# A two-layer decoder trunk on one core: a fourth buffer for split weights, embedding products in another bank, a new order of the attention steps

## The chip, the cores and the metric

The kernel runs on one core of a Trainium2 chip. The metric is the device time of one execution in microseconds (us). The engines of the core are TensorE (PE, its weight loads PEld), VectorE (DVE), ScalarE (ACT), GpSimd (POOL) and SyncE (SP, which issues the DMAs).

## The reference, cut to what matters

Two layers over 256 tokens of width 1024. Each is a feed-forward block, a mixer, a second feed-forward block and a gated embedding; the mixer of layer 0 is stick-breaking attention with 16 heads of 64, that of layer 1 a causal pooling over windows of 2, 4, 8 and 16 tokens.

```
for i in range(DEPTH):
    x = x + 0.5 * swiglu(rms_norm(x, norm_ffn1[i]), w_ffn1_gu[i], w_ffn1_down[i])
    h = rms_norm(x, norm_mix[i])
    mix = stick_breaking_attention(h, ...) if i % 2 == 0 else multiscale_pool_mixer(h, ...)
    x = x + mix
    x = x + 0.5 * swiglu(rms_norm(x, norm_ffn2[i]), w_ffn2_gu[i], w_ffn2_down[i])
    gate = jax.nn.sigmoid(rms_norm(x, norm_ple[i]) @ w_ple_gate[i])
    x = x + gate * (p[i] @ w_ple_proj[i])
```

All inputs are float32. Attention takes, for each query, scores z of the earlier keys, the running sum of log sigmoid(-z) from the key to the query, and weights exp(log sigmoid(z) + that sum).

## The kernel before

Activations lie with features on partitions: `x` is 8 chunks of 128 features by 256 tokens, inside the tile `gx`. Every float32 operand of a matmul is split into a high part (rounded to fp32r) and a low part (the rest), and each product is three matmuls, high x high, high x low and low x high (`mm3`, L183). So the weights must be split on the chip.

**The stream of weights.** All weights are cut into 163 units of 128 x 2048 floats (1 MB), in the order of use. `load(u)` (L122) fetches unit u into one of three `raw` buffers, from SP's queue. `divide(u)` (L139) makes its parts `wh` (on ScalarE, or on DVE for the first pieces where the table `SPLIT` says so) and `wl` (raw minus wh, on DVE, or on POOL for the last pieces where the table says so). The table's triple is (pieces, pieces whose `wh` is made by DVE, pieces whose `wl` is made by POOL); a unit without an entry has (2, 0, 0), which is pieces of 1024 columns. The pool `wpool` (L89) has three buffers each for `wh` and `wl`. `unit(u)` (L166) is called by whoever uses a unit: it issues loads up to u + 3 and the divisions of u and u + 1. `ahead()` (L174) issues the division of the unit two behind the newest in use. A division's instructions can run only when a buffer is free, that is when PE has used up the unit that held it.

**The order of the work.** PE and SP run in the order of the program. The instructions of ScalarE, DVE and POOL are put in an order by the compiler's own scheduler when the kernel is built, by readiness and priority; marked parts have high priority, the divisions do not. On the chip each engine then runs its instructions in that order.

**PSUM.** Eight banks: four named `mm`, two `z`, one `st`, one `o`. `next_bank()` (L106) takes every third from `z`, the others from `mm`.

**Feed-forward** (`ffn`, L400). Units 0 to 21 of a block hold gate and up weights, one pair of 128 columns each: 48 matmuls of 256 columns a unit (`project`). `gated` (L412) scales by the norm's factor `r`, takes silu and product on ScalarE and DVE, and splits the result into `hx`. The last 11 units are the down projection. From the second block on the first two units are worked on side by side, chunk by chunk of the incoming `x` (`Opening`, L346), so that PE can begin before the last chunk is ready; `statistics()` (L311) then takes the sum of squares `acc` through PE (parts `ah` and `al` into bank `st`) and makes `r`. The second block of layer 1 gets an opening of one unit, which `pooling` has begun.

**Attention** (`attention`, L463). The list `HEADS` (L70) is PE's order, written by hand: q, k, v steps are six matmuls of 512 columns each of a projection (group of heads, then chunk); T is the transposition of the queries and keys of a pair of heads into bank `st`, read out into `kh`, `kl`, `qh`, `ql`; C the scores into both `z` banks, after which ScalarE and DVE make the softplus `spv` and its parts `sph` and `spl`; S the running sums on PE, after which the weights `pwv`, `pwh`, `pwl` are made; G the sum of the values into bank `o`, read out into `oh` and `ol`; W one input chunk of the output projection (24 matmuls of 256 columns, into all four `mm` banks); E a quarter of layer 0's embedding product `p @ w_ple_proj` (12 matmuls) into bank `st`, copied into `proj` by ScalarE (L756); N the token statistics; A a call of `ahead()`. A group of k is normalized into `y` (L518) before T can use it.

**Units.** Layer 0: feed-forward 0 to 32; attention 33 to 49, of which W0 and W1 use 45, E 46, W2 to W7 use 47 to 49; feed-forward 50 to 82; embedding gate 83 to 86 (`embed`, L762). Layer 1: feed-forward 87 to 119; embedding product 120; pooling 121 to 125; feed-forward 126 to 158; gate 159 to 162. Only feed-forward, the gate and one place each in attention and pooling call `ahead()`.

Of the kernel before, what the change touches and what calls it, by code (L numbers as in the profile page):

```python
# [16 lines left out]
P = 128  # L17
D = 1024
S = 256
# [36 lines left out]
}  # L56


# [11 lines left out]
HEADS = """  # L70
q00 q01 q02 q03 q04 q05 N q06 q07 k00 k01 k02 k03 k04 k05 k06 k07
v00 v01 v02 v03 T0 v04 v05 C0 v06 T1 v07 q10 q11 S0 q12 q13 C1 G0 q14 T2 q15 q16 q17 S1
k10 k11 C2 G1 k12 T3 k13 k14 k15 S2 k16 k17 C3 G2 v10 v11 v12 v13 T4 S3 v14 v15 v16 C4 G3
v17 T5 W0 S4 E0 C5 G4 W1 T6 E1 S5 E2 C6 G5 W2 T7 W3 S6 E3 C7 G6 W4 W5 S7 W6 A G7 W7
"""


# [1 line left out]
def trunk(ctx: ExitStack, tc: tile.TileContext, gxT, pT, wts, outT):  # L79
# [39 lines left out]

    raw, split = {}, {}  # L120

    def load(u):  # L122
        if u >= UNITS or u in raw:
            return
        t = wpool.tile([P, UNIT], F32, tag="raw", name=name("raw"))
        if u == 0:
            for a, b in FIRST:
                lo, hi = (G_COLS if a else 0) + a * S, G_COLS + b * S
                nc.sync.dma_start(gx[:, lo:hi], gxT[:, lo:hi])
                c = slice(a * UNIT // 8, b * UNIT // 8)  # L130
                nc.sync.dma_start(t[:, c], wts[u, :, c])
        else:
            pieces = 4 if u == 1 else 1
            n = UNIT // pieces
            for i in range(pieces):
                nc.sync.dma_start(t[:, i * n : (i + 1) * n], wts[u, :, i * n : (i + 1) * n])
        raw[u] = t

    def divide(u, only=None):  # L139
        if u >= UNITS or (u in split and only is None):  # L140
            return
        load(u)
        if u not in split:
            split[u] = (
                wpool.tile([P, UNIT], F32R, tag="wh", name=name("wh")),
                wpool.tile([P, UNIT], F32R, tag="wl", name=name("wl")),
            )
        h, lo = split[u]
        pieces, on_dve, on_pool = SPLIT.get(u, (2, 0, 0))
        cuts = [(i * UNIT // pieces, (i + 1) * UNIT // pieces) for i in range(pieces)]  # L150
        if u == 0:
            cuts = [(a * UNIT // 8, b * UNIT // 8) for a, b in FIRST]
        for i, (a, b) in enumerate(cuts):
            if only not in (None, i):
                continue
            c = slice(a, b)
            if i < on_dve:
                nc.vector.tensor_copy(h[:, c], raw[u][:, c])
            else:
                nc.scalar.activation(h[:, c], raw[u][:, c], AF.Copy)  # L160
            eng = nc.gpsimd if i >= len(cuts) - on_pool else nc.vector
            eng.tensor_sub(lo[:, c], raw[u][:, c], f(h[:, c]))  # L162
# [10 lines left out]

    def ahead():  # L174

        divide(newest[0] + 2)

    def tile_of(u0, i):
        h, lo = unit(u0 + i // 16)
# [220 lines left out]
    def ffn(n, u0, last_norm, aside=None, before=None, opening=None):  # L400

        if n:
            opening = opening or Opening(u0, (xh, xl), list(range(NC)))
        opened = len(opening.banks) if n else 0
        if n:
            opening.step()
            statistics()
        with tc.tile_pool(name=name("ffn"), bufs=1) as pool:
            hx = pool.tile([P, 2, NFF, S], F32R, name=name("hx"))
            hh, hl = hx[:, 0], hx[:, 1]  # L410

            def gated(j, ps):  # L412
                s = tmp.tile([P, S], F32, tag="s", name=name("s"))
                nc.vector.tensor_mul(s, ps[:, :S], r)  # L414
                nc.scalar.activation(s, s, AF.Silu)
                nc.vector.tensor_mul(s, s, ps[:, S:])
                nc.scalar.activation(hh[:, j], s, AF.Copy)
                nc.vector.tensor_sub(hl[:, j], s, f(hh[:, j]))

            waiting = list(enumerate(opening.banks)) if n else []  # L420
            for w in waiting:
                gated(*w)
            waiting = []
            for j in range(opened, NFF):
                ps = next_bank()
                if u0 + j == 0:
                    for k in range(NC):
                        for i in range(2):
                            mm3(
                                ps[:, i * S : (i + 1) * S], tile_of(0, 2 * k + i),  # L430
                                (xh[:, k], xl[:, k]), i + k == 0, k == NC - 1,
                            )
                else:
                    project(u0 + j, ps, (xh, xl))
                waiting.append((j, ps))
                if n == 0 and j == 1:
                    before()
                    statistics()
                if n or j:
                    for w in waiting:  # L440
                        gated(*w)
                    waiting = []
                ahead()
                if j == 4 and aside is not None:
                    aside()
            r_ffn = r
            begin_norm()
            for d in range(NC):
                ps = next_bank()
                for k in range(NFF):  # L450
                    w = tile_of(u0 + NFF, d * NFF + k)
                    mm3(ps[:, :S], w, (hh[:, k], hl[:, k]), k == 0, k == NFF - 1)
                t = tmp.tile([P, S], F32, tag="s", name=name("s"))
                with tc.high_priority():
                    nc.vector.scalar_tensor_tensor(
                        out=t, in0=ps[:, :S], scalar=0.5, in1=r_ffn, op0=ALU.mult, op1=ALU.mult
                    )
                    nc.vector.tensor_add(x[:, d], x[:, d], t)  # L458
                    last_norm(d, d == 0)
        return u0 + UNITS_FFN  # L460


    def attention(u0, layer, embedding):  # L463
        uo = (u0 + 12, u0 + 14, u0 + 15, u0 + 16)
        with tc.tile_pool(name=name("attn"), bufs=1) as pool:
# [151 lines left out]
            for step in HEADS.split():  # L617
                what, n = step[0], step[1:]
                if what in "qkv":
                    group = "qkv".index(what) + 3 * int(n[0])  # L620
                    k = int(n[1])
                    if k == 0:
                        banks = [bank("mm"), bank("mm")]
                    project_tokens(u0 + 2 * group, banks, (k,))
                    if k == NC - 1 and what == "v":
                        c = slice(int(n[0]) * 512, int(n[0]) * 512 + 512)
                        keep_tokens(vh[:, :, c], vl[:, :, c], banks, rc)
                    elif k == NC - 1:
                        normalize((what, int(n[0])), banks, epsms)
                elif what == "N":  # L630
                    rc, epsms = token_scales()
                elif what == "A":
                    ahead()
                elif what == "E":
                    embedding(int(n), tag="st")
                else:
                    {"T": transpose, "C": scores, "S": stick, "G": gather, "W": w_o}[what](int(n))
            begin_norm()
# [99 lines left out]

    def embedding_of(u0, pool):

        proj = pool.tile([P, NC, S], F32, name=name("proj"))

        def some(*which, tag=None):
            for i in which:
# [53 lines left out]
    with tc.manual_schedule(engines={mybir.EngineType.PE, mybir.EngineType.SP}):  # L798
# [6 lines left out]
        for layer in range(DEPTH):  # L805
# [19 lines left out]
                2 * layer, u, norm_after(1, layer, ("ffn1", layer)), aside,  # L825
                None if layer else rest_of_squares,
            )
            with tc.tile_pool(name=name("embed"), bufs=1) as pool:
                if layer == 0:
                    proj, embedding = embedding_of(u + 13, pool)  # L830
                    u, opening = attention(u, layer, embedding), None
                else:
                    proj, embedding = embedding_of(u, pool)
                    u, opening = pooling(u, layer, embedding)
                u = ffn(
                    2 * layer + 1, u, norm_after(3, layer, ("ffn2", layer)), opening=opening
                )
                if layer + 1 < DEPTH:
                    u = embed(u, proj, norm_after(0, layer + 1, ("ple", layer)))
                else:  # L840
                    u = embed(u, proj, None)
        assert u == UNITS


# [93 lines left out]
```

## Time and profile before

| what | us |
|---|---|
| median of 3 runs | 1008.12 (1006.88 to 1009.69) |
| the profiled execution | 1007.78 |
| its span in the trace | 1006.1 |

All times in a trace row are microseconds from the start of the span, unless marked ns. The profiled execution is 1.7 us longer than its span, which is the work around it. A group of instructions is named by line, engine, operation and tiles, out<-in; since the matmuls are recorded by one helper, all of them have line L111. In the timeline a bracket names the idle time ahead of an instruction and what ended it.

### The profile page before, as it was taken

What the parts mean: (1) busy time and instruction counts of PE and PEld (TensorE: products, weight loads), DVE (VectorE), ACT (ScalarE), POOL (GpSimd) and SP (SyncE); (2) the same over time, 40 slices, a digit from 0 to 9 for tenths busy, and PEclk for the clock granted to TensorE, in tenths of its full rate; (3) what the DMA queues carried; (4) which work ended last, traced back from release to release, by engine and by line L of the source; (5) the groups of instructions that cost most, each with busy time, mean ns of one, the idle gap of its engine ahead of it and who ended that gap; (6) DMA issues with size and microseconds to landing.
All of it is one profiled execution on the core that took longest, in us unless ns stands there. A gap on an engine that the chain in (4) does not pass through costs nothing.

```text
span 1006.1 us, 18488 instructions
## 1 busy us (share of the span) xinstructions
PE 977.6 (97%) x7710; PEld 951.6 (95%) x7710; DVE 670.5 (67%) x1107; ACT 527.6 (52%) x885; POOL 122.5 (12%) x183
## 2 busy tenths in 40 slices
PE   8999999999998999999999999999999899999997
PEld 8999999987777999999999999999998899999997
DVE  7966565678966876565658676565666766565565
ACT  5654544457756674444438554443456654444442
POOL 4300002500000000000240070000220000000262
PEclk9999999999989999999999999999999999999999
DMA  7754554543321364555543555555554355545531
GB/s 252 262 209 169 198 178 171 208 168 125 129 100 66 133 238 176 192 186 188 189 175 121 209 212 177 189 188 184 194 174 162 126 203 175 193 184 189 190 126 42
DMA packets 26292, 174.77 MB, mean 174 GB/s; under 512 B 2912, under 2 KB 3680, under 8 KB 5600
## 3 DMA queue, kind: packets, MB, share of 16 engines
q1 hardware_dynamic: 26208, 173.59, 48.1%
q8 instruction: 60, 0.98, 0.4%
q14 instruction: 24, 0.20, 0.1%
HBM read 172.53 MB, written 1.05 MB: 173 GB/s over the span
## 4 chain that ended last, share of the span: by engine, by line
PE 92%; DVE 5%; ACT 2%; issue 1%; DMA 1%; SPq 0%; DVEq 0%
PE mm L111 61%; PE z L111 29%; DVE wl L162 1%; PE st L111 1%; DMA gx<-gxT 1%; PE o L111 1%; DVE xx L278 0%; ACT wh L160 0%; ACT spv L566 0%; ACT spv L565 0%; DVE acc L287 0%; DVE ql L547 0%; ACT spv L567 0%; DVE gx L695 0%; PE st L532 0%
## 5 line engine op out<-in xcount | busy, mean ns | idle before, releaser
L160 ACT ACTIVATE wh<-raw 128x1024 fp32r<-128x1024 f32 (+2 forms) x428 | 346.7, 840 | 308.7 <-PE mm L111 164.3
L162 DVE TENSOR_TENSOR wl<-raw,wh 128x1024 fp32r<-128x1024 f32 (+2 forms) x401 | 385.8, 980 | 107.4 <-ACT wh L160 106.5
L111 PE MATMUL mm<-xx,wh 128*128 128x256 f32 x1984 | 354.1, 280 | 0.2 <-DVE xx L278 0.2
L111 PEld LDWEIGHTS mm<-xx,wh 128*128 128x128 f32 x1984 | 304.2, 188 | 0.4 <-DVE xx L278 0.4
L111 PE MATMUL mm<-xx,wl 128*128 128x256 f32 x992 | 278.1, 280 | 3.1 <-DVE wl L162 3.1
L111 PE MATMUL z<-xx,wh 128*128 128x256 f32 x1088 | 198.2, 283 | 2.1 <-ACT wh L160 1.4
L111 PEld LDWEIGHTS mm<-xx,wl 128*128 128x128 f32 x992 | 186.9, 188 | 3.5 <-DVE wl L162 3.5
L111 PE MATMUL mm<-hx,wh 128*128 128x256 f32 x968 | 172.3, 281 | 0.0
L111 PEld LDWEIGHTS z<-xx,wh 128*128 128x128 f32 x1088 | 169.5, 191 | 2.5 <-ACT wh L160 1.6
L111 PE MATMUL z<-xx,wl 128*128 128x256 f32 x544 | 153.7, 283 | 0.9 <-DVE wl L162 0.9
L111 PEld LDWEIGHTS mm<-hx,wh 128*128 128x128 f32 x968 | 148.4, 188 | 0.0
L111 PE MATMUL mm<-hx,wl 128*128 128x256 f32 x484 | 136.0, 281 | 0.0
L111 PEld LDWEIGHTS z<-xx,wl 128*128 128x128 f32 x544 | 104.0, 191 | 1.1 <-DVE wl L162 1.1
L111 PEld LDWEIGHTS mm<-hx,wl 128*128 128x128 f32 x484 | 91.2, 188 | 0.0
L289 POOL TENSOR_TENSOR acc<-gx 128x256 f32<-128x256 f32 x5 | 3.1, 612 | 649.2 <-DVE gx L458 647.0
L111 PE MATMUL mm<-wh,xx 128*128 128x512 f32 x240 | 81.2, 403 | 0.0
L111 PE MATMUL z<-hx,wh 128*128 128x256 f32 x440 | 78.5, 281 | 0.0
L414 DVE TENSOR_TENSOR s<-mm,r 128x256 f32<-128x256 f32 x57 | 24.0, 423 | 77.6 <-PE mm L111 77.4
L111 PEld LDWEIGHTS z<-hx,wh 128*128 128x128 f32 x440 | 67.5, 188 | 0.0
L277 ACT ACTIVATE xx<-gx 128x256 fp32r<-128x256 f32 x64 | 31.3, 504 | 61.5 <-DVE gx L458 52.6
L111 PE MATMUL z<-hx,wl 128*128 128x256 f32 x220 | 61.8, 281 | 0.0
L162 POOL TENSOR_TENSOR wl<-raw,wh 128x512 fp32r<-128x512 f32 (+1 forms) x34 | 57.1, 1700 | 36.2 <-ACT wh L160 31.9
(204 smaller groups left out, 1015.9 us busy)
## 6 DMA issues: line engine op xcount, KB each, us to landing
raw<-wts SPq DMA_DIRECT2D x161, 1024.0 KB, 4.8
raw<-wts SPq DMA_DIRECT2D x7, 256.0 KB, 6.2
gx<-gxT SPq DMA_DIRECT2D x3, 256.0 KB, 5.6
outT<-gx SPq DMA_DIRECT2D x3, 256.0 KB, 2.6
p<-pT SPq DMA_DIRECT2D x2, 256.0 KB, 2.6
raw<-wts SPq DMA_DIRECT2D x2, 128.0 KB, 2.7
outT<-gx SPq DMA_DIRECT2D x2, 128.0 KB, 1.9
gx<-gxT SPq DMA_DIRECT2D x1, 165.0 KB, 2.2
```

Of the source, the lines that this page charges most:

```text
L111: nc.tensor.matmul(out, lhsT, rhs, start=start, stop=stop, skip_group_check=True)
L160: nc.scalar.activation(h[:, c], raw[u][:, c], AF.Copy)
L162: eng.tensor_sub(lo[:, c], raw[u][:, c], f(h[:, c]))
L277: high = nc.scalar.activation(xh[:, d], x[:, d], AF.Copy, scale=gc)
L289: nc.gpsimd.tensor_mul(acc, x[:, d], x[:, d])
L414: nc.vector.tensor_mul(s, ps[:, :S], r)
```

## The change

A second pool, `wpool4`, is opened when attention is done, with one more buffer each for `wh` and `wl`; from then on every fourth division takes it, and `ahead()` issues the divisions two and three behind the newest unit. To make room below it, the pool of `proj` is kept open from layer 0's attention to the end and used by both layers. The entries of `SPLIT` for 26 units from 83 on are taken out, so that these have two pieces, all `wh` on ScalarE and all `wl` on DVE. Embedding's products in attention go into bank `o`. `HEADS` is reordered in its last rows. In a block with an opening of one unit, the statistics and the gating of that unit come after the second unit's matmuls.

```diff
@@ SPLIT
-    81: (4, 1, 3), 82: (4, 0, 4), 83: (4, 1, 0), 84: (4, 1, 0), 85: (4, 0, 0), 86: (4, 0, 0),
-    87: (4, 0, 0), 88: (4, 0, 0), 89: (4, 0, 0), 90: (4, 0, 0), 91: (4, 0, 0), 117: (2, 0, 1),
-    119: (2, 0, 1), 120: (4, 0, 1), 121: (4, 0, 0), 122: (4, 0, 0), 123: (4, 0, 0),
-    124: (4, 0, 0), 125: (4, 0, 0), 126: (4, 0, 0), 127: (4, 0, 0), 129: (4, 0, 0),
-    130: (4, 0, 0), 131: (4, 0, 0), 156: (4, 0, 0), 157: (2, 0, 1), 158: (2, 0, 1),
-    159: (2, 0, 1), 160: (4, 1, 2), 161: (4, 0, 4), 162: (4, 0, 4),
+    81: (4, 1, 3), 82: (4, 0, 4), 117: (2, 0, 1), 119: (2, 0, 1), 156: (4, 0, 0),
@@ HEADS
-k10 k11 C2 G1 k12 T3 k13 k14 k15 S2 k16 k17 C3 G2 v10 v11 v12 v13 T4 S3 v14 v15 v16 C4 G3
-v17 T5 W0 S4 E0 C5 G4 W1 T6 E1 S5 E2 C6 G5 W2 T7 W3 S6 E3 C7 G6 W4 W5 S7 W6 A G7 W7
+k10 k11 C2 G1 k12 T3 k13 k14 k15 S2 k16 k17 C3 G2 v10 v11 v12 S3 v13 v14 v15 T4 v16 C4 G3
+v17 T5 W0 S4 E0 C5 G4 W1 T6 E1 S5 E2 C6 G5 W2 T7 E3 S6 W3 C7 G6 W4 S7 W5 A G7 W6 W7
@@ trunk
+    fourth, turns = [], [0]
@@ divide
-            split[u] = (
-                wpool.tile([P, UNIT], F32R, tag="wh", name=name("wh")),
-                wpool.tile([P, UNIT], F32R, tag="wl", name=name("wl")),
+            turns[0] += len(fourth)
+            home = fourth[0] if turns[0] % 4 == 3 else wpool
+            split[u] = tuple(
+                home.tile([P, UNIT], F32R, tag=n, name=name(n)) for n in ("wh", "wl")
             )
@@ ahead
-        divide(newest[0] + 2)
+        for i in range(1 + len(fourth)):
+            divide(newest[0] + 2 + i)
@@ ffn
             opening.step()
-            statistics()
+            if opened > 1:
+                statistics()
...
-            for w in waiting:
-                gated(*w)
-            waiting = []
+            if opened > 1:
+                for w in waiting:
+                    gated(*w)
+                waiting = []
...
-                if n == 0 and j == 1:
-                    before()
+                if j == 1 and opened < 2:
+                    if n == 0:
+                        before()
                     statistics()
-                if n or j:
+                if j:
@@ attention
-                    embedding(int(n), tag="st")
+                    embedding(int(n), tag="o")
@@ embedding_of
-        proj = pool.tile([P, NC, S], F32, name=name("proj"))
+        proj = pool.tile([P, NC, S], F32, tag="proj", name=name("proj"))
@@ the loop over the layers
-            with tc.tile_pool(name=name("embed"), bufs=1) as pool:
-                if layer == 0:
-                    proj, embedding = embedding_of(u + 13, pool)
-                    u, opening = attention(u, layer, embedding), None
...
+            if layer == 0:
+                pool = ctx.enter_context(tc.tile_pool(name="embed", bufs=1))
+                proj, embedding = embedding_of(u + 13, pool)
+                u, opening = attention(u, layer, embedding), None
+                fourth.append(ctx.enter_context(tc.tile_pool(name="wpool4", bufs=1)))
```

## Rows read from the trace of the kernel before

**Rows 1.** The page, part 1: busy time, share of the span, instructions.

```profile
PE 977.6 (97%) x7710; PEld 951.6 (95%) x7710; DVE 670.5 (67%) x1107; ACT 527.6 (52%) x885; POOL 122.5 (12%) x183
```

**Rows 2.** Windows view, 357:528, 562:742 and 800:975 taken together, busy us.

```profile
sum 526.00, PE 526.00 PEld 526.00 DVE 327.24 ACT 248.66 POOL 71.70; mean PE 175.33 PEld 175.33 DVE 109.08 ACT 82.89 POOL 23.90
```

**Rows 3.** The chain inside feed-forward: start us, us, what.

```profile
398.21 11.31 PE mm L111 x96
```

**Rows 4.** Waits of PE: waited for, us in total, times, longest us.

```profile
PE st L111 <- DVE ql L547: 5.5, 2, 4.3
PE mm L111 <- DVE wl L162: 3.1, 2, 2.0
PE st L532 <- DVE y L518: 3.0, 2, 2.8
PE st L111 <- ACT ah L318: 1.4, 1, 1.4
...
PE st L111 <- DVE al L319: 0.5, 1, 0.5
```

**Rows 5.** Windows view: busy us (x instructions), granted clock, DMA share, GB/s.

```profile
274.00:278.00 4.00, 1.12 (x6) 0.47 (x5) 3.97 (x10) 2.19 (x4) 0.00 (x0) 0.87 0.36 111
278.00:284.00 6.00, 6.00 (x17) 4.94 (x18) 3.85 (x9) 2.04 (x5) 0.00 (x0) 0.52 0.73 276
307.00:312.00 5.00, 4.51 (x23) 4.46 (x24) 1.07 (x3) 1.23 (x3) 0.00 (x0) 0.66 0.61 210
337.00:342.00 5.00, 3.94 (x31) 3.74 (x32) 3.24 (x9) 2.64 (x9) 0.00 (x0) 1.00 0.59 210
556.00:561.00 5.00, 4.97 (x29) 4.97 (x30) 4.78 (x10) 2.63 (x5) 0.00 (x0) 0.66 0.80 283
792.00:796.00 4.00, 3.59 (x17) 3.59 (x18) 2.30 (x6) 3.77 (x6) 0.00 (x0) 0.57 0.58 240
...
534.00:552.00 18.00, 18.00 (x155) 18.00 (x154) 16.09 (x32) 15.19 (x32) 0.00 (x0) 1.00 0.34 117
```

**Rows 6.** PE's timeline in attention: start us, us, instruction [idle before <-releaser].

```profile
277.40 1.07 PE L532 MATMUL st<-ident,y 128*128 128x128 f32 x2 [2.76 <-DVE y L518]
285.90 0.28 PE L111 MATMUL z<-qh,kh 128*128 128x256 f32 x1
295.92 0.35 PE L111 MATMUL st<-eh,wh 128*128 128x256 f32 x1 [1.16 <-DVE ql L547]
307.49 0.39 PE L111 MATMUL st<-eh,wh 128*128 128x256 f32 x1 [4.35 <-DVE ql L547]
314.03 0.28 PE L111 MATMUL z<-mask,ident 128*128 128x256 f32 x1
324.82 0.28 PE L111 MATMUL z<-mask,ident 128*128 128x256 f32 x1
337.98 0.39 PE L111 MATMUL mm<-oh,wh 128*128 128x256 f32 x1 [1.33 <-ACT oh L602]
```

**Rows 7.** DVE's timeline in attention and at the opening of layer 1.

```profile
282.98 0.43 DVE L547 TENSOR_TENSOR ql<-st,qh 64x256 fp32r<-64x256 f32 x1 [0.45 <-ACT qh L546]
306.92 0.43 DVE L547 TENSOR_TENSOR ql<-st,qh 64x256 fp32r<-64x256 f32 x1
318.44 0.69 DVE L572 TENSOR_TENSOR spl<-spv,sph 128x512 fp32r<-128x512 f32 x1
330.76 0.68 DVE L572 TENSOR_TENSOR spl<-spv,sph 128x512 fp32r<-128x512 f32 x1
552.03 1.28 DVE L162 TENSOR_TENSOR wl<-raw,wh 128x512 fp32r<-128x512 f32 x2
```

**Rows 8.** The page, part 5: the splits by engine, busy, mean, idle before.

```profile
L160 ACT ACTIVATE wh<-raw 128x1024 fp32r<-128x1024 f32 (+2 forms) x428 | 346.7, 840 | 308.7 <-PE mm L111 164.3
L162 DVE TENSOR_TENSOR wl<-raw,wh 128x1024 fp32r<-128x1024 f32 (+2 forms) x401 | 385.8, 980 | 107.4 <-ACT wh L160 106.5
...
L162 POOL TENSOR_TENSOR wl<-raw,wh 128x512 fp32r<-128x512 f32 (+1 forms) x34 | 57.1, 1700 | 36.2 <-ACT wh L160 31.9
```

More of the change, by code (lines that the diff above doesn't have):

```diff
@@ L827, in trunk @@
             )
-            with tc.tile_pool(name=name("embed"), bufs=1) as pool:
-                if layer == 0:
-                    proj, embedding = embedding_of(u + 13, pool)
-                    u, opening = attention(u, layer, embedding), None
[L832 to L841, printed above, removed]
+            if layer == 0:
[3 more added lines that the diff above has]
+                fourth.append(ctx.enter_context(tc.tile_pool(name="wpool4", bufs=1)))
+            else:
+                proj, embedding = embedding_of(u, pool)
+                u, opening = pooling(u, layer, embedding)
+            u = ffn(2 * layer + 1, u, norm_after(3, layer, ("ffn2", layer)), opening=opening)
+            if layer + 1 < DEPTH:
+                u = embed(u, proj, norm_after(0, layer + 1, ("ple", layer)))
+            else:
+                u = embed(u, proj, None)
         assert u == UNITS
```

## The prediction

> **What bounds the kernel now.** I read the page's first part, then three long stretches of the windows view, the chain, PE's waits, and the timelines around the waits. The first says that the matmul engine is busy 97% of the span [rows 1]; since overlapping matmuls are counted as busy, that alone proves little. The windows view settles it: the middles of the last three long feed-forward stretches, 526 us in all, have 526 us of PE busy, while DVE is busy 62% of it [rows 2]. There one row of the chain gives the price of a matmul: 96 in 11.31 us, 0.118 us each [rows 3]. Nothing but fewer matmuls would shorten these stretches, and the change removes none. So the room is in the transitions, and PE's waits list them [rows 4]: 5.5 us for `ql`, 3.1 us for `wl`, 3.0 us for `y`, 1.4 and 0.5 us for `ah` and `al`; one of 1.33 us for `oh` comes up under D. Behind four of them stands a second bill: the granted clock is 0.52 in 278 to 284 us, 0.66 in 307 to 312, 0.66 in 556 to 561, 0.57 in 792 to 796, against 1.00 after the shorter wait at 338 [rows 5]. These are stretches in which part of the matmuls run at 1.2 GHz rather than 2.4. I price each as its length times the missing share: 6.0 x 0.48 = 2.9 us, 5.0 x 0.34 = 1.7, 1.7 again, and 4.0 x 0.43 = 1.7.
>
> **The change, part by part.** The sum is made against the profiled execution, 1007.78 us (its span is 1006.1); the median of the runs shown is 0.34 us above it, which I add at the end.
>
> *A. T4 behind S3, v13, v14, v15.* PE stands 2.76 us at T4's transposes, waiting for `y`, and then has the slow 278 to 284 us [rows 5, 6]: 5.7 us. Between T4 and C4 there were S3, v14, v15, v16; now there is v16 alone, six matmuls of twice 256 columns, 1.4 us. So the wait for `y` is filled with 1.4 + 4.2 us of other work, but C4 comes close behind T4, and what is late next is C4's `ql`. In the kernel before the last `ql` of T4 starts at 282.98 [rows 7] and ends near 283.4, 4.9 us after T4's last matmul, and C4 starts at 285.90 [rows 6]. Bounds of the gain: 0 if C4 waits until PE has lost all again, 5.7 if T4's chain shrinks into v16. DVE was busy 3.97 of the 4 us from 274 to 278 [rows 5], so `ql` can come at best a little sooner; C4 near 283.4 is 2.5 us better. I take 2.5.
>
> *B. E0 into bank `o`.* In `st` its first matmul waits until T5's `ql` has read the bank, 1.16 us [rows 6]. `o` was emptied after G3, long before. C5, which needs that `ql` too, then starts as E0's 12 matmuls end (1.4 us). Gain 1.2. The copy of the product (one ScalarE instruction of 128x512, taken as no dearer than the mean split piece, 0.84 us [rows 8]) must now leave `o` before G4; C5's scores lie between (five matmuls of 256 and three of 512 columns, 1.3 us) and cover it. If that cover went, G4 would wait up to 0.8 us.
>
> *C. E1 into bank `o`.* It waited 4.35 us for T6's last `ql`, which starts at 306.92 [rows 6, 7], and the slow stretch behind it cost 1.7: 6.05 in all. Now E1, S5 and E2 (1.4, 0.9 for four matmuls of 256 and two of 512 columns, 1.4) run in that gap, and only C6 needs the `ql`. From the end of T6 (307.49 - 4.35 = 303.1) to the end of that `ql` (307.4) are 4.3 us, the three pieces fill 3.7; 0.6 stays. Gain 5.5, bounds 3.7 (the clock falls all the same, 0.6 stays) to 6.05.
>
> *D. W6 between G7 and W7, S7 before W5.* W7 waited 1.33 us for G7's `oh` [rows 6]; W6's 24 matmuls (2.8 us) now cover it: +1.3. But S7 stands only G6 (three of 256, three of 512: 1.1 us) and W4 (2.8) behind C7, 3.9 us; before, W5 lay between as well. From the last score matmul to the last `spl` C6 took from 314.2 to 319.1, 4.9 us, and C7, with split pieces between, from 325.0 to 331.4, 6.4 us [rows 6, 7]. So S7 waits 1.0 to 2.5 us less what its first four matmuls (0.5 us) do beforehand. I take 0.6, the uncontended row, since the order of these engines follows PE's: net +0.7, bounds -0.8 to +1.3.
>
> *E. The fourth buffer at the first embedding gate.* ScalarE and DVE start a unit's split as soon as the third unit back has been consumed; with a fourth pair of buffers it is the fourth back, one unit (48 matmuls, 5.65 us) earlier. At the opening of layer 1's first FFN two units are consumed side by side, and their `wl` pieces are late: 3.1 us in two waits, 1.7 us of slow clock [rows 4, 5]. DVE is busy 16.09 of the 18 us before [rows 5], so pieces with low priority come last; the last `wl` of the first of the two units ends near 552.7 [rows 7], and the second unit's pieces come after it, up to the 556 at which the slow stretch begins. With the shift the second unit takes the place of the first, some 3 us earlier. Gain 4.0 of 4.8, bounds 1.5 and 4.8.
>
> *F. Statistics after the second gate pair at the second FFN of layer 1.* PE stood for `ah` and `al` (1.4 + 0.5 us [rows 4]), then slow clock, 1.7. Now 48 matmuls (5.65 us) of the next unit come first. The gating of two banks is late by that; six banks rotate, so three are still free. Gain 3.3 of 3.6; below zero only if that next unit's split were late, which the fourth buffer makes unlikely.
>
> *Edits costed at nothing.* 26 units lose their entry, most of them 4 pieces that become 2: two 512-wide `wl` take 1.28 us together [rows 7], and one of twice the width is taken as the same. What POOL did of them, 4.25 units, goes to DVE: a piece took POOL 57.1 / 34 = 1.7 us, DVE 0.98 [rows 8]; 17 pieces of 512 columns at 0.64 are 10.9 us of DVE work, nearly all in the last feed-forward, where DVE is 38% free [rows 2]. Three DVE copies go to ScalarE, 0.84 us each at the mean. All of it is covered by the 5.65 us a unit that PE needs; uncovered, a piece blocks the in-order DVE for 1.3 us where it was 0.64. The loads stay the same in number and order on SP's queue. `proj` kept throughout and the fourth pair placed where attention's tiles were cost a wait at most once, for tiles already read.
>
> *H. A new short wait.* The first FFN's second unit after attention is split only once W5 is done; then came W6, S7, G7 and W7, now G7, W6 and W7 (1.1 + 2.8 + 2.8 = 6.7 us). I set 1.0 against this and the coarser pieces; bounds 0 and 4.8, the price of such lateness in E.
>
> Sum: 2.5 + 1.2 + 5.5 + 0.7 + 4.0 + 3.3 - 1.0 = 16.2; 1007.78 - 16.2 + 0.34 = 991.9, say 992. If every wait named vanished with its slow stretch: 5.7 + 1.2 + 6.05 + 1.3 + 4.8 + 3.6 = 22.6, so 985.8 is the floor.
>
> **The rivals.**
>
> *Waits halve, the clock falls all the same.* For it: waits of 1.4 and 0.5 us were enough ahead of the 0.57 stretch [rows 4, 5], and the new waits at C4 and S7 follow DVE's full stretch. Against it: the 1.33 us at 338 left the clock at 1.00 [rows 5]. Then A gives 0, B 1.2, C 3.7, D -0.8, E 2.3, F 1.9, H -1.0: 7.3, or 1000.8. The Trainium skill bears on this (TensorE: Matmul & The Clock Gate, "HAM oscillation"): the throttled clock is the default and activity releases it, so matmul bursts between waits pay it again after each. By that rule this rival's time is the one to expect; the row at 338 shows a wait that paid nothing.
>
> *E is not relieved.* DVE's load before the embedding gate is the same per unit and only shifts; if its high-priority work again pushes the low pieces behind, E gives 0, and the time is 996.
>
> *The change doesn't do what it says.* If the divisions wait for raw weights rather than for buffers, nothing comes earlier, and B to D trade waits among themselves: 1008. Against it: the splits on ScalarE waited 164.3 us for PE [rows 8], so buffers are what they lack.
>
> *Slower: the deeper look-ahead in ScalarE's queue.* Every step of the FFN now offers two units to split. If the compiled order puts a split that waits for PE ahead of the gating work, what is queued behind it on ScalarE is late, banks are not freed, and PE waits in every unit. From unit 50 on there are 113; at 0.2 us each that is 22.6 us, 1014. It decides from (16.2 + 3) / 113 = 0.17 us per unit. Against it: in 526 us of the same loop PE shows no loss [rows 2].
>
> **How the numbers follow.** The forecast has 0.60, the clock rival 0.20, E unrelieved 0.09, no effect 0.05, slower 0.06. About 0.3% (3 us) is what a measurement of this kernel can tell from no change. Faster is 0.60 + 0.20 + 0.09 = 0.89, same 0.05, slower 0.06. The range runs from 986, the floor, to 1001, the clock rival's time; outside are the last two cases and a part of the rival's.
>
> **What would show it.** Right: no PE wait over 1 us on `st` with embedding operands; C4 rather than T4 as the wait near 282; no `wl` wait at layer 1's opening; no wait on `ah`; full clock in the four stretches. Wrong: waits on `wl` inside the feed-forward stretches, or PE busy below their length; a wait over 2.5 us at S7; a granted clock still near 0.6 behind waits that have halved.

## The result: 13 us faster

The kernel after takes 994.62 us (median of 4 runs, 994.5 to 996.94), the kernel before beside it 1007.5 (4 runs, 1001.3 to 1009.69): a ratio of 0.9887 [0.9841, 0.9934]. The forecast was 992.0, the range 986 to 1001. The profiled executions are 1007.78 and 994.74 us, their spans 1006.1 and 993.0; where these 13.1 us come from is the subject of what follows.

The page of the kernel after, part 1:

```profile
PE 974.0 (98%) x7710; PEld 947.8 (95%) x7710; DVE 666.3 (67%) x1072; ACT 524.5 (53%) x842; POOL 99.3 (10%) x169
```

The matmuls are the same 7710 [rows 1]. PE's waits after, longest first (what is waited for, us in total, times, longest us); the start-up has the two on `wl` and `wh`:

```profile
PE z L106 <- ACT qh L548: 3.1, 3, 1.8
PE z L106 <- DVE wl L160: 1.9, 2, 1.5
PE z L106 <- DVE spl L574: 1.6, 2, 0.9
PE z L106 <- ACT wh L158: 1.4, 2, 1.0
...
PE st L534 <- DVE y L520: 0.8, 3, 0.3
...
PE mm L106 <- DVE pl L679: 0.5, 1, 0.5
...
PE o L106 <- ACT proj L758: 0.2, 1, 0.2
```

Against [rows 4], the waits of `st` on `ql`, `ah` and `al` are gone, as is that of `mm` on `wl`; those on `qh` and `spl` took their place. PE's timeline in attention shows where (start, us, instruction, the wait in brackets):

```profile
283.18 0.38 PE L106 MATMUL z<-qh,kh 128*128 128x256 f32 x1 [1.13 <-ACT qh L548]
...
305.66 0.39 PE L106 MATMUL z<-qh,kh 128*128 128x256 f32 x1 [1.78 <-ACT qh L548]
...
323.38 0.39 PE L106 MATMUL z<-spl,tri 128*128 128x256 f32 x1 [0.67 <-DVE spl L574]
...
325.18 0.50 PE L106 MATMUL z<-spl,tri 128*128 128x512 f32 x1 [0.94 <-DVE spl L574]
```

These are C4, C6 and two places inside S7. The windows view of the stretches around the waits (busy us of each engine, then the granted clock, DMA share, GB/s):

```profile
276.00:284.00 8.00, 6.26 (x28) 4.33 (x27) 6.67 (x15) 3.43 (x7) 0.00 (x0) 1.00 0.58 178
306.00:312.00 6.00, 5.92 (x45) 5.63 (x45) 3.50 (x9) 3.60 (x9) 0.00 (x0) 1.00 0.26 109
320.00:326.00 6.00, 4.30 (x29) 3.54 (x29) 5.22 (x12) 3.23 (x8) 0.00 (x0) 0.99 0.54 194
326.00:332.00 6.00, 6.00 (x37) 5.86 (x36) 2.50 (x5) 2.35 (x6) 0.00 (x0) 0.73 0.37 153
540.00:552.00 12.00, 12.00 (x104) 12.00 (x103) 11.01 (x21) 9.01 (x18) 0.00 (x0) 1.00 0.24 87
770.00:790.00 20.00, 19.54 (x165) 19.28 (x165) 17.50 (x32) 14.90 (x26) 0.00 (x0) 1.00 0.44 158
```

The four slow stretches of [rows 5] are at full clock; a new one, 0.73, with part of its matmuls at 1.2 GHz rather than 2.4, stands behind S7's two waits.

To place the time I cut PE's timeline into stages, each from the start of one matmul to that of another, the same matmuls in every kernel. Differences to before, in us:

| stage | before | after | difference |
|---|---|---|---|
| start to layer 0's first down projection | 135.31 | 135.92 | +0.6 |
| T0 to W0 | 63.76 | 60.89 | -2.9 |
| W0 to the end of W7 | 51.17 | 48.94 | -2.2 |
| end of W7 to the down projection | 124.73 | 125.25 | +0.5 |
| embedding gate and opening of layer 1 | 39.43 | 34.38 | -5.1 |
| first feed-forward of layer 1 up to its down projection | 113.30 | 113.84 | +0.5 |
| pooling up to the last down projection | 169.52 | 164.82 | -4.7 |
| each of the three later down projections | 62.36 | 62.54 | +0.2 each |
| the last gates | 23.35 | 22.95 | -0.4 |

Behind the last matmul nothing changes, so these make the 13.1 us (13.04 unrounded). The start-up's +0.6 says nothing of the change: no edit reaches that stage, and in the kernels below it takes 135.2 to 138.2 us. So four places gain 14.9 us and long stretches without a single wait lose 1.6. The chain shows how (start us, us, what): most units still take 5.65 us, some 5.76, and 132 matmuls of a later down projection take 15.66 to 15.69, where the same chain of the kernel before has 15.62.

```profile
410.99 11.31 PE mm L106 x96
422.30 5.76 PE z L106 x48
...
456.43 5.65 PE z L106 x48
462.08 15.68 PE mm L106 x132
```

### The profile page after: what moved, and what is told of

Its sections match the earlier page's. It is cut to its first block, busy times and chain, and to the rows that moved or that the text cites. A ratio compares the mean times of both kernels' runs of the same rounds, so it can differ in the third digit from the quotient of the medians.

```text
span 993.0 us, 18385 instructions
## 1 busy us (share of the span) xinstructions
PE 974.0 (98%) x7710; PEld 947.8 (95%) x7710; DVE 666.3 (67%) x1072; ACT 524.5 (53%) x842; POOL 99.3 (10%) x169
## 4 chain that ended last, share of the span: by engine, by line
PE 93%; DVE 4%; ACT 2%; DMA 1%; issue 0%; SPq 0%; DVEq 0%
PE mm L106 62%; PE z L106 29%; DVE wl L160 1%; PE o L106 1%; DMA gx<-gxT 1%; ACT wh L158 1%; DVE ql L549 0%; DVE pwl L589 0%; ACT qh L548 0%; DVE pwh L588 0%; DVE spv L570 0%; PE st L106 0%; DVE spl L574 0%; ACT spv L568 0%; ACT spv L567 0%
## 5 line engine op out<-in xcount | busy, mean ns | idle before, releaser
L158 ACT ACTIVATE wh<-raw 128x1024 fp32r<-128x1024 f32 (+2 forms) x385 | 342.5, 916 | 299.6 <-PE mm L106 159.9
L106 PEld LDWEIGHTS mm<-wh,xx 128*128 128x128 f32 x240 | 45.2, 188 | 10.3
```

Of the source, the lines that this page charges most:

```text
L106: nc.tensor.matmul(out, lhsT, rhs, start=start, stop=stop, skip_group_check=True)
```

## The experiments

All edits are to the kernel after unless said otherwise. Ratios are to the kernel before on the same chip, with 95% intervals; a kernel of one run has only its stages, from its trace. In these kernels a stage that an edit doesn't reach repeats within 0.1 us, the start-up excepted, as long as the granted clock in it is the same.

**Without the fourth buffer.**

```diff
-                fourth.append(ctx.enter_context(tc.tile_pool(name="wpool4", bufs=1)))
```

> The changed kernel with three buffers for split units throughout and a look-ahead of two; all its other edits stay. Theory (term E: the fourth buffer alone relieves the opening of layer 1): PE waits for wl or wh pieces at layer 1's first opening, 3 to 5 us, with a slow clock stretch of 1.5 to 2 us behind, and perhaps smaller ones at the pooling block and the last gate, since the pieces are coarser than before: 999 to 1003 us, 5 to 8 above the changed kernel's 994.6. Rival (the new cutting of the units or POOL's relief did it): 993 to 996, no wait there.

1000.04 us, 0.9909 [0.9894, 0.9924], span 997.0. The edit takes out the deeper look-ahead together with the buffer; the two were not run apart. One wait of 3.8 us stands at layer 1's opening, whose stage takes 41.20 us against 34.38. From PE's waits of this kernel, and from its windows view behind the wait:

```profile
PE mm L106 <- DVE wl L160: 3.8, 1, 3.8
...
551.00:558.00 7.00, 6.14 (x28) 6.14 (x29) 4.88 (x8) 2.93 (x6) 0.00 (x0) 0.52 0.51 183
```

The fourth buffer is worth 6.8 us there. That is 1.8 more than the kernel before shows (41.20 against 39.43): its wait was 0.7 us shorter, and the slow clock behind it cost 1.7 us [rows 5] against 7 us x 0.48 = 3.4 here, which more than covers it. That the coarser cuts make the wait longer is likely, but no run changes them alone. And the buffer doesn't give the span 6.8: every later gate stretch and down projection is faster without it, the one at 113.84 back at 113.30, each 62.54 back at 62.36. So the buffer, or its place, is what makes some units 5.76 us.

**Statistics ahead of the second gate unit again.**

```diff
-            if opened > 1:
-                statistics()
+            statistics()
```

The gating of the opened unit goes back ahead in the same way.

> The changed kernel with the statistics and the gating of the opened unit ahead of the second unit again, in the second feed-forward block of layer 1. Theory (term F: the postponement alone removed the wait for ah and al): a PE wait of 1.5 to 2.5 us on bank st before the second unit, and a slow stretch of up to 1.7 us: 997 to 999 us. Rival (the earlier splits had already freed DVE there, so the sum of squares would now be in time): a wait under 0.5 us, 994.5 to 995.5.

996.58 us, 0.9875 [0.9856, 0.9894], span 994.5. The wait on `al` is back at 0.4 us alone, and pooling takes 165.76, 0.9 more. The postponement by itself is worth 0.9 us, so something else had removed most of the 4.7. The four runs don't resolve 0.9 us; the figure is the stage's.

**The old order from T7 on.**

```diff
-... G5 W2 T7 E3 S6 W3 C7 G6 W4 S7 W5 A G7 W6 W7
+... G5 W2 T7 W3 S6 E3 C7 G6 W4 W5 S7 W6 A G7 W7
```

> The changed kernel with the old order of the last steps of attention from T7 on (W3 S6 E3 C7 G6 W4 W5 S7 W6 A G7 W7). Theory (term D was wrong: S7 close behind C7 now costs more than W7's wait did): the waits at S7, 1.6 us, and the 0.73 clock of 326 to 332 go, W7's wait of 1.3 us comes back: 992 to 993.5 us, 1 to 2.5 below the changed kernel. Rival (term D as forecast): 995 to 996 us.

993.7 us, 0.9847 [0.9829, 0.9864], span 990.4. The profiled execution is faster than the kernel after's; the interval overlaps that kernel's, and of the four runs two take 992.2 and 992.7 us at a mean granted clock of 0.997, two 994.7 and 995.0 at 0.993. In the trace S7's waits are gone, the one on `oh` is back with the 1.3 us of [rows 6], and the clock stays full behind it. From PE's waits of this kernel:

```profile
PE mm L106 <- ACT oh L604: 1.3, 1, 1.3
```

And from its windows view, the stretch in which that wait lies:

```profile
326.00:332.00 6.00, 4.60 (x34) 3.92 (x33) 4.03 (x9) 2.30 (x6) 0.00 (x0) 1.00 0.74 249
```

W0 to W7 falls from 48.94 to 46.95. In these two traces the new tail costs 2.0 us, most of it by the slow clock; what is left of the new order and the bank gains 51.17 - 46.95 = 4.2.

**Embedding's products in bank `st`, as before.**

```diff
-                    embedding(int(n), tag="o")
+                    embedding(int(n), tag="st")
```

> The changed kernel with the embedding products in bank st again. Theory (terms B and C: the bank alone made E0 and E1 wait): waits of 1 to 1.5 us at E0 and 3 to 4.5 us at E1 return, C6's wait of 1.8 us goes, a slow stretch of about 1.7 us comes behind E1: 998 to 1001 us. Rival (the waits came from late split pieces in front of ql on DVE and fall on C5 and C6 in either bank): 994.5 to 996 us.

1002.02 us, 0.9928 [0.9911, 0.9945], span 1001.1. Three products wait for `ql`, and the clock falls. From PE's waits:

```profile
PE st L106 <- DVE ql L549: 8.4, 3, 4.4
```

And the windows view around the second of the three, 4.4 us long:

```profile
300.00:306.00 6.00, 1.64 (x10) 1.43 (x9) 4.61 (x9) 3.39 (x7) 0.00 (x0) 0.82 0.18 45
306.00:312.00 6.00, 6.00 (x32) 5.77 (x31) 1.84 (x4) 1.97 (x5) 0.00 (x0) 0.61 0.39 162
```

W0 to W7 takes 57.48, 8.5 more. In the new order the bank is worth 8.5 us: the third of the waits, 2.9 us, is E3's directly behind T7, so the order needs the bank.

**T4 in its old place.**

```diff
-v12 S3 v13 v14 v15 T4 v16 C4
+v12 v13 T4 S3 v14 v15 v16 C4
```

> The kernel after with the fifth transposition group back in its old place, behind S3, v13, v14 and v15. Theory (A): TensorE waits 2.8 us ahead of T4 again, the stretch from T0 to W0 takes 63.8 us instead of 60.9, the granted clock falls below 0.9 in the stretch behind the wait, and the span is 993.0 + 2.9 = 995.9 us. Rival (the fall of the clock comes from the attention steps' own short matmuls, not from the wait): the stretch is within 0.5 us of 60.9.

996.19 us in one run, span 994.5. The wait is the old one, but T0 to W0 takes 62.54, not 63.8: the stretch behind the wait has the clock at 0.72, where the kernel before had 0.52 [rows 5]. PE's timeline of this kernel, at T4:

```profile
277.76 0.33 PE L534 MATMUL st<-ident,y 128*128 128x128 f32 x1 [2.76 <-DVE y L520]
```

Its windows view, behind T4:

```profile
278.00:284.00 6.00, 5.73 (x22) 4.78 (x22) 4.21 (x10) 2.05 (x5) 0.00 (x0) 0.72 0.75 299
```

The order gives 1.65 us; 6 us x 0.20 = 1.2 us of the 2.9 are a difference in the clock that the same wait brought, which I can't attribute. Further on this kernel has the kernel after's waits at C6 (1.74 us) and in S7 (0.67 + 0.94), but its clock falls behind C6 and not behind S7:

```profile
306.00:312.00 6.00, 4.87 (x20) 4.24 (x21) 2.67 (x8) 3.71 (x9) 0.00 (x0) 0.73 0.41 167
329.00:335.00 6.00, 6.00 (x50) 5.87 (x50) 4.04 (x8) 3.10 (x7) 0.00 (x0) 1.00 0.37 157
```

From T7 to the end of W7 it takes 23.88 us; the kernel after, with the same steps and the same waits, takes 25.40, the old tail 23.34. So of the 2.0 us that the new tail costs in the kernel after, 0.5 are the tail itself and 1.5 the clock.

**The old cuts, and the old cuts with the statistics ahead.** The 26 entries of `SPLIT` come back; in the second kernel the edit of the statistics above as well.

> The changed kernel with the table of cuts of the kernel before. Theory (the coarser cuts and POOL's relief cost and gain nothing by themselves, as forecast): every stage within 0.5 us of the changed kernel. Rival (with four pieces DVE's queue is again full of short splits in pooling and at layer 1's opening): the pooling stretch, 164.8 us in the changed kernel, is 1 us longer or more.

> The changed kernel with the old table of cuts and with the statistics ahead of the second unit. With the new cuts, the statistics ahead cost only 0.9 us (165.8 against 164.8 us for the pooling stretch; 169.5 in the kernel before). Theory (the cuts removed most of the wait for ah and al): the pooling stretch is 168 to 170 us and PE waits 1.5 to 2.5 us on bank st. Rival (the earlier splits of the fourth buffer did): 165.5 to 166.5 us, wait under 0.6 us.

997.54 us (span 995.8) and 1000.05 (998.3), one run each. Some 2 us of both lie in the start-up stage (138.19 and 138.03 us), which the edit doesn't reach. Of the rest, the first differs from the kernel after by +0.5 at the last gates (23.45); every other stage is within 0.1. The second has pooling at 165.94 and a wait on `ah` of 0.5 us, a third of [rows 4]. From PE's waits of the second:

```profile
PE st L111 <- ACT ah L322: 0.5, 1, 0.5
```

Its stage from W0 to W7 takes 50.50 us, 1.6 more than after's, with the same waits: 1.79 us at C6 and 0.67 + 0.94 in S7. Its windows view shows why. Behind C6 the clock is at 0.72, and 6 us x 0.28 = 1.7; the kernel after had 1.00 there. Behind S7's pair it falls in both. The row behind C6:

```profile
306.00:312.00 6.00, 4.14 (x14) 3.46 (x15) 2.89 (x8) 3.42 (x7) 0.00 (x0) 0.72 0.51 178
```

So with the fourth buffer the cuts hardly matter, and with old cuts and old statistics the buffer brings pooling from 169.52 to 165.94.

**Three buffers, statistics ahead, new cuts.** Both edits, of the first and the second experiment.

> The kernel after with three buffers only and the statistics again ahead of the second gate unit; the coarser cuts stay. In the kernel before, the end of the pooling stretch waited 1.4 us on ah and 0.5 on al, and the stretch took 169.5 us; with either the fourth buffer or the postponement alone it was 164 to 166. Theory (either of the two suffices, the cuts do nothing): without both, the waits on ah and al come back and the stretch takes 168 to 170 us; the opening of layer 1's first feed-forward 41 us, as in e1_no_fourth; a span of about 997.0 + 5 = 1002 us. Rival (the cuts or the pieces moved to VectorE had removed it): the stretch stays at 164 to 166 and the span at 997 to 998.

1000.13 us in one run, span 998.4, at the rival's end. Pooling takes 165.21; the waits are small, while the one at layer 1's opening is there in full, as PE's waits show:

```profile
PE mm L106 <- DVE wl L160: 3.8, 1, 3.8
...
PE st L106 <- DVE al L318: 0.4, 1, 0.4
...
PE st L106 <- ACT ah L317: 0.2, 1, 0.2
```

My theory that the cuts do nothing fell: without buffer and postponement they bring pooling from 169.52 to 165.21, as the buffer does without the other two to 165.94. A kernel with none of the three but with attention's edits was not run, so the kernel before stands in for it. Either removes the same lateness; the postponement adds 0.9 with the buffer and 1.3 without (163.87 in the first experiment).

**W in halves, T6 and T7 one step earlier.** W5 and W6 are split between S7, A and G7.

```diff
-... G4 W1 T6 E1 S5 E2 C6 G5 W2 T7 E3 S6 W3 C7 G6 W4 S7 W5 A G7 W6 W7
+... G4 T6 W1 E1 S5 E2 C6 G5 T7 W2 E3 S6 W3 C7 G6 W4 W5a S7 W5b W6a A G7 W6b W7
```

> The changed kernel with the output projection's steps cut in halves (a: the first four output chunks, b: the others), and T6 and T7 ahead of W1 and W2: G4 T6 W1 E1 S5 E2 C6 G5 T7 W2 E3 S6 W3 C7 G6 W4 W5a S7 W5b W6a A G7 W6b W7. Theory (what is left in attention is C6 close behind T6 and S7 close behind C7): C6's wait of 1.8 us goes, S7's two waits fall from 1.6 us to under 0.5 and the slow stretch behind them goes, W7 waits under 0.5 us; W0 to W7 takes 43 to 45 us rather than 48.9: 989 to 991. Rival (DVE and ScalarE are the bound there, so the waits only move to the next step): 47 to 49 us, 993 to 995.

989.53 us, 0.9832 [0.9783, 0.9881], span 987.8. C6's wait is gone and S7's is 0.3; W0 to W7 falls by 5.1 to 43.81, and the clock stays full. PE's waits:

```profile
PE z L106 <- ACT qh L548: 1.3, 2, 1.1
...
PE o L106 <- DVE ol L605: 0.4, 1, 0.4
PE z L106 <- DVE spl L574: 0.3, 1, 0.3
```

The windows view of the stretch in which the kernel after has S7's waits and the slow clock:

```profile
320.00:326.00 6.00, 5.67 (x46) 5.30 (x45) 5.15 (x11) 2.83 (x7) 0.00 (x0) 1.00 0.47 191
326.00:332.00 6.00, 5.92 (x45) 5.40 (x45) 4.35 (x11) 3.18 (x9) 0.00 (x0) 1.00 0.61 202
```

**Where the tiles lie.** Nothing in the traces of before and after waits inside the slower units, so I looked at the layout: the three old pairs of buffers lie where they were, the fourth pair begins at byte 167328 of a partition, and `hx`, which was there, now begins at 183712. Unused bytes shift both: 32 ahead of the embedding's tiles, or 64; and 32 ahead and 32 behind the fourth pair, on top of the halves.

```diff
                 pool = ctx.enter_context(tc.tile_pool(name="embed", bufs=1))
+                pool.tile([P, 8], F32, tag="pad", name="pad")
```

> The changed kernel with an unused tile of 32 bytes a partition ahead of the embedding tile, so that the fourth pair begins at byte 167360 of a partition, a multiple of 64 as the other three pairs do, rather than at 167328. In the changed kernel each unit held by the fourth pair takes PE 5.76 rather than 5.65 us, about 10 ns more on each second wl matmul. Theory (the address modulo 64 bytes is the cause): all units take 5.65 us, the stretch from the end of attention to the down projection falls from 125.25 to 124.7 us, some 2.6 us over the program: 991.5 to 992.5. Rivals (the far place of the pair in the memory, or wh and wl lying side by side): nothing moves, 994 to 995.5.

> The kernel after with 64 free bytes, not 32, ahead of the embedding's tiles: the fourth pair of tiles stands at byte 167392, the feed-forward's tile of products at 183776; both keep the remainder by 64 that they have in the kernel after (32 and 32). Theory (the remainder by 64 decides): the stages are those of the kernel after, 125.25 us for the gate units behind attention and 62.54 for each later down projection, span 993.0 within 0.5. Rival (any other shift changes the pace, a larger modulus): the gate units take 124.7, or the down projections another time than 62.54.

> The W steps in halves as in e6_halves, and in addition 32 free bytes ahead of the fourth buffer and 32 behind it: the fourth buffer's pair of tiles stands at byte 167360 of a partition, as in e5_align, and the feed-forward's tile of products keeps its remainder of 32 bytes by 64 that it had in the kernel after. Theory (the place of an operand sets the pace of the matmuls that read it): the second attention half's gate units take 124.3 us rather than 124.83, the gate units of layer 1's first feed-forward 113.3 rather than 113.84, the pooling stretch 164.3 rather than 164.84, and the three later down projections 62.36 each rather than 62.54; the sum is 987.8 - 0.5 - 0.5 - 0.5 - 0.5 = 985.8 us of span, a time of 987.5 us. Rival (the pace hangs on what else moves at that time, and e5 only happened to shift it): the stages stay as in e6_halves or go as in e5_align, with down projections of 63.24 us, a span of 988 or more.

The 32 bytes alone: 995.99 us, 0.9896 [0.9854, 0.9938], span 993.4, where 991.5 to 992.5 was expected: the units of 5.76 us are gone, but the down projections are slower. The 64 bytes: 990.45 us in one run, span 988.7. The halves with both pads: **985.12 us** (984.15 to 986.83), 0.9768 [0.9749, 0.9788], span 982.7, the fastest of all and 9.5 us below the kernel after; its down projections are faster than expected. The bytes are where the program puts the tiles when it is built. Their stages:

| kernel | fourth pair at | `hx` at | layer 1's gate stretch | each later down projection |
|---|---|---|---|---|
| before | none | 167328 (159136 in layer 1's first block) | 113.30 | 62.36 |
| without the fourth buffer | none | 167328 | 113.30 | 62.36 |
| after; also the halves | 167328 | 183712 | 113.84 | 62.54 |
| 32 bytes | 167360 | 183744 | 113.31 | 63.24 |
| halves, 32 and 32 bytes | 167360 | 183776 | 113.31 | 61.48 |
| 64 bytes | 167392 | 183776 | 113.25 | 61.96 |

In the chain, the later down projections' groups of 132 take nearly the same time within a kernel, and those of layer 0's first block, whose `hx` is at 159136 in every kernel, always 15.62. One later row of the 32 bytes:

```profile
461.61 15.84 PE mm L106 x132
```

One of the halves with both pads:

```profile
456.29 15.40 PE mm L106 x132
```

One of the 64 bytes (its last two groups take 15.50 and 15.48):

```profile
460.87 15.56 PE mm L106 x132
```

The gate stretch goes with the place of the fourth pair, the down projections mostly with that of `hx`: with the pair at 167360, 32 bytes more for `hx` make 63.24 into 61.48; with `hx` at 183776, 32 bytes more for the pair make 61.48 into 61.96 (the halves by themselves leave 62.54 as it was). The same 132 matmuls without a wait take 15.40 to 15.84 us, 2.9% apart. My rule, the remainder by 64, failed: the 64 bytes keep both remainders, and the kernel was to stay at 993; it gained 4.3 us. Nor is the place of the operands all. The 96 matmuls of the opening behind attention have their operands at the same bytes in the kernel after, the halves, the halves with both pads and the 64 bytes, and run at full clock. Yet in the chain six of them take 0.71 us in the kernel after:

```profile
336.95 0.71 PE z L106 x6
```

and 0.71 again in the halves with both pads, but 0.68 in the halves and with the 64 bytes. One row of the 64 bytes:

```profile
336.69 0.68 PE z L106 x6
```

What rule there is, and by what mechanism, stays open.

## Why the prediction was right, and where it was not

Direction and size were right; several terms were not, and they cancelled in part, so that a total within 3 us of the forecast is in part luck. The floor of the sum is 985.5 us, not 985.8.

| term | forecast | measured | by |
|---|---|---|---|
| A, T4 | 2.5 | 2.9, of which order 1.65 | the stage; T4 put back |
| B, E0 in bank `o` | 1.2 | 1.3 | W0 to T6, the old tail against before |
| C, E1 and E2 in bank `o` | 5.5 | 2.9 | T6 to W7, the old tail against before |
| D, the tail | +0.7 | -2.0, of which clock 1.5 | the old tail against after; T4 put back |
| E, layer 1's opening | 4.0 | 5.05 | the stage |
| F, pooling | 3.3 | 4.7, of which the postponement 0.9 | the stage; statistics ahead |
| last gates, from the cuts | 0 | 0.4 to 0.5 | the stage; the old cuts |
| H, a new wait | -1.0 | no wait; -1.6 by slower units | the stages |

With -0.6 from the start-up the measured column is the 13.1 us.

**A** held as argued: C4, not T4, is what is late next, with 1.13 us and full clock. But the order shows 1.65 of the 2.5 forecast; the rest of the 2.9 is the difference in the clock.

**B** held. In **C** the step that failed is the end of T6's last `ql`: I left it 4.3 us behind T6, as in the kernel before, and filled the gap with E1, S5 and E2. But the filling has work of its own on DVE. ScalarE's timeline of the kernel after:

```profile
302.03 0.87 ACT L587 ACTIVATE pwv<-z 128x256 f32<-128x256 f32 x2
302.77 0.37 ACT L548 ACTIVATE qh<-st 64x256 fp32r<-64x256 f32 x1
303.92 0.60 ACT L758 ACTIVATE proj<-o 128x512 f32<-128x512 f32 x1 [0.77 <-PE o L106]
305.23 0.38 ACT L548 ACTIVATE qh<-st 64x256 fp32r<-64x256 f32 x1 [0.71 <-DVE ql L549]
```

DVE's in the same stretch:

```profile
303.31 0.62 DVE L588 CAST pwh<-pwv 128x256 fp32r<-128x256 f32 x2
303.85 1.02 DVE L589 TENSOR_TENSOR pwl<-pwv,pwh 128x256 fp32r<-128x256 f32 x2
304.78 0.41 DVE L549 TENSOR_TENSOR ql<-st,qh 64x256 fp32r<-64x256 f32 x1
305.64 0.43 DVE L549 TENSOR_TENSOR ql<-st,qh 64x256 fp32r<-64x256 f32 x1 [0.45 <-ACT qh L548]
```

S5's `pwh` and `pwl`, some 1.6 us, stand in DVE's queue ahead of the first `ql`, and ScalarE's second `qh` comes only behind that `ql`. The copy of E2's product, also between the two `qh`, costs nothing: ScalarE idles 0.71 us after it until the `ql` is done. C6 starts at 305.66 after 1.78 us, where I had 0.6. With T6 one W earlier, in the halves, this wait is gone.

**D** has the wrong sign. I gave S7 a wait of 0.6 us, by the quicker of two rows, and left out the clock: it was 0.67 + 0.94, and the 0.73 behind it is another 6 us x 0.27 = 1.6. The bound of -0.8 was too near, as it held no clock; the 0.5 us that the tail costs at full clock lies inside it.

**E** was the right mechanism, undersized by 1 us: the whole wait and its slow stretch went. **F** named the waits rightly but credited the wrong edit. The cuts, which I costed at nothing, and the fourth buffer each remove most of the lateness; only 0.9 belongs to the postponement.

**H** is the step that was missing altogether: I looked for a wait. The loss is in the pace of matmuls that wait for nothing. That nothing but fewer matmuls would shorten the long stretches was wrong, too: with the halves and both pads 132 of them take 15.40 us where the kernel before has 15.62. No row of before showed that the pace can change.

Of the rivals, *E is not relieved* and *no effect* fell with the opening at 34.38 us. *The deeper look-ahead* fell too: no unit waits inside the feed-forward. *The clock falls all the same* was right at one place of the kernel after, but the place is not fixed. There the waits of 1.13 and 1.78 us had the clock at 1.00 behind them, the pair of 0.67 and 0.94 had 0.73. With T4 in its old place it was C6's 1.74 us that had 0.73, and the same pair 1.00; with the old cuts and statistics both had a slow stretch. By the Trainium skill (TensorE: Matmul & The Clock Gate, "HAM oscillation") bursts between waits, in a kernel with longer waits, pay the slow clock again. The traces agree for the E waits in bank `st` (0.82 and 0.61), for the pair and for C6 in some kernels and not in others, and not for C4. What tells these apart the runs don't show; a wait of 1 to 2 us in attention can cost its own length or, with some 1.6 us of slow clock, twice that.

The clock is also a good part of the gain. Priced as in the prediction, it cost the kernel before 2.9 + 1.7 + 1.7 + 1.7 = 8.0 us and the kernel after 1.6, so some 6 of the 14.9 us, an estimate. And it varies from one execution to the next: the kernel before took 1000.7 us at a mean granted clock of 0.991 and 1010.5 at 0.984 in its runs beside the experiments.

## What to carry to other kernels

Work moved into a wait to fill it also puts its own splits into the queues of the engines that are waited for: price the filling on those engines too, and start the late chain earlier rather than fill behind it. When several edits aim at one stretch, undo each alone and two together, since either of two may be enough and the one meant for it may do least. After moving a large tile, compare the time of a run of matmuls that wait for nothing before looking for waits, and try a few dozen bytes of padding. A difference of 1 to 2 us between two traces can be the clock alone: compare the granted clock behind the same wait before crediting an edit.

## What was not expected of the hardware

The same row of 132 matmuls without waits, at full clock, took 15.40, 15.56, 15.68 or 15.84 us with `hx` and the fourth pair of weights in places 32 to 64 bytes apart; a unit of 48 took 5.65 us, or 5.76 with its weights at 167328. Over the kernel this was worth 4.3 us with 64 unused bytes, and on top of the better order 987.8 - 982.7 = 5.1 us of span, of which 0.6 lie in the start-up. Each padded place is one trace. Also, the same wait was followed by different granted clocks: 2.76 us at T4 by 0.52 or 0.72, some 1.8 us at C6 by 1.00 or 0.72, the pair in S7 by 0.73 or 1.00.
